# Five weight tiles carried together through the first normalization of a two-block transformer kernel

## The chip, the cores and the metric

One core of one Trainium2 chip runs the whole kernel as one launch. The metric is the device time of that launch in microseconds (us). The core's engines each work through their own queue in order: TensorE (PE, matmuls; PEld is its weight load), VectorE (DVE), ScalarE (ACT), GpSimd (POOL), and SyncE (SP), which issues the DMA transfers.

## The reference, cut to what matters

Two transformer blocks follow each other. The change touches only the entry of the first one: a vector `mod` of six parts is made from the condition `c`, two parts of it (`shift1`, `scale1`) turn the normalized input into `h`, and `h` is multiplied by the wide matrix `w_in`.

```python
mod = jax.nn.silu(c) @ w_ada[l] + b_ada[l]
shift1, scale1, gate1, shift2, scale2, gate2 = jnp.split(mod[:, None, :], 6, axis=-1)
h = rms_norm(x, norm1_w[l]) * (1 + scale1) + shift1
proj = h @ w_in[l]
(dn_q, dn_k, dn_v, dn_z, dn_alpha, dn_beta,
 mla_q, mla_ckv, mla_kr, gate_dn, gate_mla) = jnp.split(proj, split_at, axis=-1)
qkv = jax.nn.silu(causal_dwconv(jnp.concatenate([dn_q, dn_k, dn_v], axis=-1), dn_conv_w[l]))
...
```

There are 512 tokens (`T`) and 1024 features (`D`); all is float32. Behind the projection come a gated delta rule, a latent attention, a feed-forward part, and the second block. They take nearly all of the time and are not edited.

## The kernel before, in words

Features lie on the 128 partitions and tokens along the free dimension, so `x` and `h` are 8 slices (`KD`) of 128x512. Every product in float32 is made of two halves: `split` lets ScalarE round a tensor to `hi` (L294) and VectorE take the rest as `lo` (L295). `mm3` (L308 to L310) then issues three matmuls per slice: hi by hi, hi by lo, lo by hi. `proj` does that for the 8 slices of one weight tile, so one tile of 128 output features is 24 matmuls into one PSUM bank. `wload` fetches a tile of 128x1024 into `raw` (two buffers) and splits it. Two PSUM banks named `mm` are used in turn by all weight tiles.

The entry (the block with `w0`) works in this order:

1. `ssx`: the sum of squares of `x` on TensorE (L428), then `rstd` on ScalarE.
2. VectorE multiplies the 8 slices of `X0` by `rstd` (L433).
3. The modulation. `scale1` for slices 0 to 3 and `shift1` for slices 4 to 7 come from `cols_` on TensorE: a row of 512 outputs (L407, the vector is the stationary operand), copied by ScalarE (L410) and turned into columns by tiny matmuls (L413). The other half comes from `rows` on VectorE: one multiply-and-sum over 128x1024 for each block of 128 outputs (L397), eight in all.
4. `modulate`: ScalarE applies scale and shift to a slice (L420) and writes its `hi`, VectorE its `lo`. Slices 0 to 3 go first, then 4 and 5, then 6 and 7. The slices together are `H`.

Only two weight tiles, number 8 and `misc` (80 columns), are loaded inside this block. The first stage behind it (`t = 0`) projects tiles 8, 9, 0, 1, 16 and 17, each followed by `conv_silu`: ScalarE copies the PSUM bank (L527), VectorE adds three shifted products read from that bank (L529), ScalarE applies SiLU. The bank is free after the third product. `misc`, `ab` and `decay` make the decay terms (`aps` L480, `gps` L500). The next stage (`pre_steps`) begins with `gb`, `kk` and `ssp` on TensorE.

The order in which each engine gets its instructions is decided by the framework's scheduler from the order of the code, the buffers and its own costs. On the chip each engine keeps that order and waits where it must.

## Time and profile before

| what | value |
|---|---|
| median of three runs | 2167.57 us (2164.92 to 2167.89) |
| the profiled execution, its own time | 2166.97 us |
| its span, first to last instruction | 2165.2 us |
| TensorE busy | 2135.2 us, 99% |
| VectorE busy | 1202.5 us, 56% |
| ScalarE busy | 898.0 us, 41% |

A busy TensorE is not one at full speed: an interval also counts as busy while slow or small matmuls run in it. The first 100 us are the part that the change touches; TensorE is busy for 87.54 us of them.

### The profile page before, as it was taken

The numbers are of one execution on the slowest core, as the hardware profiler recorded it, in microseconds if no ns is written. First come the engines' busy times: TensorE is split into PE (matmuls) and PEld (weight loads), VectorE is DVE, ScalarE is ACT, GpSimd is POOL, SyncE is SP. The second block draws the span as 40 slices with busy tenths as digits, with TensorE's granted clock in tenths as the row PEclk, the third lists the DMA queues.
The fourth block names the chain that finished last, engine by engine and source line by source line (L and its number), as shares of the span: only waits on it lengthen the run. The fifth ranks groups of instructions, "written<-read, shape, count | busy, mean of one in ns | idle before, by whom it ended". The sixth has DMA issues, their size and how long they took to land.

```text
span 2165.2 us, 27498 instructions
## 1 busy us (share of the span) xinstructions
PE 2135.2 (99%) x10636; PEld 1722.0 (80%) x10636; DVE 1202.5 (56%) x2243; ACT 898.0 (41%) x1479; POOL 17.8 (1%) x49
## 2 busy tenths in 40 slices
PE   7999999999999999999999999999999999999997
PEld 3787877778888878888888887887778888888886
DVE  4777667465554554444335898545544454334446
ACT  5645443465553353333224323634443343224333
POOL 1000000000000000000000000000000000000000
PEclk9999999999999999999999999999999999999999
DMA  8533334222224343333333222232222433333332
GB/s 312 167 109 115 90 91 131 61 67 69 73 71 129 105 136 94 96 95 95 95 100 117 80 83 83 74 98 83 84 78 82 148 97 98 96 98 97 92 96 77
DMA packets 89579, 219.86 MB, mean 102 GB/s; under 512 B 23384, under 2 KB 28648, under 8 KB 88808
## 3 DMA queue, kind: packets, MB, share of 16 engines
q1 hardware_dynamic: 89448, 218.10, 33.0%
q8 instruction: 84, 1.38, 0.3%
q14 instruction: 47, 0.39, 0.1%
HBM read 211.50 MB, written 7.08 MB: 101 GB/s over the span
## 4 chain that ended last, share of the span: by engine, by line
PE 90%; DVE 5%; ACT 2%; issue 1%; DMA 1%; SPq 0%; DVEq 0%; ACTq 0%
PE mm L308 25%; PE mm L310 25%; PE mm L309 24%; PE pp L689 2%; DVE yc L1265 1%; DVE lo L295 1%; PE bpo L1593 1%; PE po L1041 1%; PE tps L1202 1%; PE tps L1203 1%; PE tps L1204 1%; PE ssp L571 1%; PE pw L762 1%; PE pc L789 1%; PE ss L779 1%
## 5 line engine op out<-in xcount | busy, mean ns | idle before, releaser
L294 ACT ACTIVATE hi<-raw 128x1024 fp32r<-128x1024 f32 (+3 forms) x354 | 351.5, 994 | 779.0 <-PE mm L309 690.4
L295 DVE TENSOR_TENSOR lo<-raw,hi 128x1024 fp32r<-128x1024 f32 (+3 forms) x354 | 403.8, 1141 | 439.0 <-ACT hi L294 427.9
L308 PE MATMUL mm<-H,hi 128*128 128x512 f32 x856 | 341.8, 400 | 4.7 <-ACT hi L294 1.7
L310 PE MATMUL mm<-H,lo 128*128 128x512 f32 (+1 forms) x856 | 340.5, 398 | 0.5 <-DVE lo L295 0.5
L309 PE MATMUL mm<-H,hi 128*128 128x512 f32 (+1 forms) x856 | 340.0, 397 | 0.0
L308 PEld LDWEIGHTS mm<-H,hi 128*128 128x128 f32 x856 | 161.4, 189 | 41.2 <-issue 3.0
L310 PEld LDWEIGHTS mm<-H,lo 128*128 128x128 f32 (+1 forms) x856 | 161.4, 189 | 36.1 <-issue 3.4
L309 PEld LDWEIGHTS mm<-H,hi 128*128 128x128 f32 (+1 forms) x856 | 161.5, 189 | 33.9 <-issue 2.7
L308 PE MATMUL mm<-XN,hi 128*128 128x512 f32 (+1 forms) x456 | 180.0, 395 | 0.0
L309 PE MATMUL mm<-XN,hi 128*128 128x512 f32 (+1 forms) x456 | 179.6, 394 | 0.0
L310 PE MATMUL mm<-XN,lo 128*128 128x512 f32 (+1 forms) x456 | 179.3, 393 | 0.0
L310 PEld LDWEIGHTS mm<-XN,lo 128*128 128x128 f32 (+1 forms) x456 | 85.1, 187 | 19.3 <-issue 1.7
L308 PEld LDWEIGHTS mm<-XN,hi 128*128 128x128 f32 (+1 forms) x456 | 85.1, 187 | 18.8 <-ACT hi L294 0.9
L309 PE MATMUL mm<-HN,hi 128*128 128x512 f32 x256 | 100.0, 391 | 0.0
L308 PE MATMUL mm<-HN,hi 128*128 128x512 f32 x256 | 99.6, 389 | 0.0
L310 PE MATMUL mm<-HN,lo 128*128 128x512 f32 x256 | 99.6, 389 | 0.0
L308 PE MATMUL mm<-F,hi 128*128 128x512 f32 x256 | 99.6, 389 | 0.0
L309 PE MATMUL mm<-F,hi 128*128 128x512 f32 x256 | 99.6, 389 | 0.0
L310 PE MATMUL mm<-F,lo 128*128 128x512 f32 x256 | 99.6, 389 | 0.0
L309 PEld LDWEIGHTS mm<-XN,hi 128*128 128x128 f32 (+1 forms) x456 | 84.9, 186 | 17.8 <-issue 1.3
L1265 DVE SCALAR_TENSOR_TENSOR yc<-cp,cdh,yc 128x512 f32<-128x512 f32 x120 | 89.9, 750 | 2.9
L308 PE MATMUL mm<-FF,hi 128*128 128x512 f32 x176 | 68.5, 389 | 0.0
(662 smaller groups left out, 3817.1 us busy)
## 6 DMA issues: line engine op xcount, KB each, us to landing
raw<-in_w_ff SPq DMA_DIRECT2D x64, 512.0 KB, 3.6
raw<-in_ffn_up SPq DMA_DIRECT2D x44, 512.0 KB, 3.6
raw<-in_w_dn SPq DMA_DIRECT2D x32, 512.0 KB, 3.8
adraw<-in_w_adaT SPq DMA_DIRECT2D x64, 256.0 KB, 3.2
raw<-in_w_ga SPq DMA_DIRECT2D x32, 512.0 KB, 3.7
raw<-in_w_br SPq DMA_DIRECT2D x32, 256.0 KB, 2.7
raw<-in_ffn_down SPq DMA_DIRECT2D x16, 448.0 KB, 3.4
X<-in_xT SPq DMA_DIRECT2D x4, 1024.0 KB, 7.2
```

The lines of the kernel that those rows point to most:

```text
L294: nc.scalar.activation(out=hi, in_=src, func=AF.Copy)
L295: nc.vector.tensor_tensor(out=lo, in0=src, in1=hi.bitcast(F32), op=ALU.subtract)
L308: nc.tensor.matmul(ps, wh, xh, start=start, stop=False)
L309: nc.tensor.matmul(ps, wh, xl, start=False, stop=False)
L310: nc.tensor.matmul(ps, wl, xh, start=False, stop=stop)
L571: nc.tensor.matmul(ssp[64 * h:64 * h + 64, kind * 8 + c:kind * 8 + c + 1], sq[:, c], C("ones", 0, 1), start=True, stop=True)
L689: nc.tensor.matmul(pp[:, c4], lh[:, c4], rh[:, c4], start=True, stop=True)
L762: nc.tensor.matmul(pw[64 * h:64 * h + 64], st["wt"][b][:, c4, 64 * h:64 * h + 64], S[:, h], start=True, stop=True)
L779: nc.tensor.matmul(ss, st["kd"][b][64 * h:64 * h + 64, c4], vn[64 * h:64 * h + 64], start=True, stop=True)
L789: nc.tensor.matmul(pc[:, 0], ATT[(2 * p + b) % 4][:, c4], vn, start=True, stop=True)
L1041: nc.tensor.matmul(po[:, qs], VT[:, kb, hh], pT[:, kb * P:kb * P + P], start=(kb == 0), stop=(kb == qb))
L1265: i = nc.vector.scalar_tensor_tensor(out=ycs[m], in0=cps[m][:, s:s + T], scalar=cdh[:, m * 31 + s:m * 31 + s + 1], in1=ycs[m], op0=ALU.mul ...
```

## The change

It edits the entry block and the beginning of stage 0.

- The five tiles `FIRST` = 8, `misc`, 9, 0, 1 are loaded and split inside the entry block, into buffers of their own (`phi`, `plo`). Each has its own PSUM bank: two are the `mm` banks, three come from a new pool `pfirst`. The loop over slices is now outside and the loop over tiles inside, so each slice of `H` is multiplied into all five tiles.
- The modulation goes pair by pair of slices: for slices k and k+1 both scale and shift, then the multiplication by `rstd`, then `H`. `scale1` of slices 0 to 3 is made on TensorE as columns at once (`on_pe`: the weight block is the stationary operand, the vector the moving one, 8 matmuls to a block). The other twelve blocks are on VectorE (`on_dve`), one DMA each.
- The row of `c` (`crow`, 512 KB once spread over the partitions) is now fetched before the constants `CS` and the second half of `x`.
- Stage 0 no longer projects these five tiles; their convolutions are called ahead of the stage, which keeps tiles 16 and 17.

```diff
-    a["w_ada1"] = np.ascontiguousarray(wa[:, T:T + D].reshape(KD, P, D).transpose(1, 0, 2))
-    a["w_adaT"] = np.ascontiguousarray(np.delete(wa.T.reshape(12, 4, P, D), (1, 2), axis=0).reshape(40, P, D))
+    a["w_ada1"] = wtiles(wa[:, D:D + T])
+    a["w_adaT"] = np.ascontiguousarray(np.delete(wa.T.reshape(12, 4, P, D), 2, axis=0).reshape(44, P, D))
...
+        if own is None:
...
+        else:
+            hi = own.tile([P, CH], F32R, tag="phi", name="phi", bufs=len(FIRST))
+            lo = own.tile([P, CH], F32R, tag="plo", name="plo", bufs=len(FIRST))
...
+    FIRST = (8, "misc", 9, 0, 1)
+    dpx = ExitStack()
+    pst = dpx.enter_context(pool("pst", 1, PS))
+    ppre = dpx.enter_context(pool("ppre", 1, PS))
+    fpx = ExitStack()
+    pfirst = fpx.enter_context(pool("pfirst", 3, PS))
...
+        cb = w0.tile([P, D], F32, name="cb0")
+        nc.sync.dma_start(out=cb, in_=A["crow"].to_broadcast([P, D]))
         nc.sync.dma_start(out=CS, in_=A["consts"])
         nc.sync.dma_start(out=X0[:, 4:8], in_=A["xT"][:, 4:8])
...
+        def ad_tile():
+            return w0.tile([P, D], F32, tag="ad", name="ad", bufs=10)
+
+        def on_dve(j, m):
+            raw = ad_tile()
+            nc.sync.dma_start(out=raw, in_=A["w_adaT"][j])
+            nc.vector.tensor_tensor_reduce(out=raw, in0=raw, in1=cb, scale=1.0, scalar=0.0,
+                                           op0=ALU.mult, op1=ALU.add, accum_out=am[:, m:m + 1])
+
+        def on_pe(k):
+            raw = ad_tile().rearrange("p (k c) -> p k c", k=KD)
+            nc.sync.dma_start(out=raw, in_=A["w_ada1"][k])
+            for kk in range(KD):
+                nc.tensor.matmul(adc[:, k:k + 1], raw[:, kk], csil[:, kk:kk + 1], start=(kk == 0), stop=(kk == KD - 1))
...
+        def first_w(i):
+            if i == "misc":
+                W0[i] = wload(A["w_misc"], KD, 80, w0)
+            else:
+                W0[i] = wload(A["w_dn"][i], KD, P, w0)
+            PS0[i] = (PSM[0] if len(PS0) < 2 else pfirst).tile([P, T], F32, tag="mm", name="mm")
...
+        for k in range(0, KD, 2):
+            for kk in (k, k + 1):
+                if kk < 4:
+                    on_pe(kk)
+                else:
+                    on_dve(4 + kk, 8 + kk)
+                on_dve(kk, kk)
+            if k == 0:
+                first_w(FIRST[0])
+                first_w(FIRST[1])
+            elif k // 2 + 1 < len(FIRST):
+                first_w(FIRST[k // 2 + 1])
+            mods(k)
+            for kk in (k, k + 1):
+                nc.vector.tensor_tensor(out=X0[:, kk], in0=X0[:, kk], in1=rstd, op=ALU.mult)
+                nc.scalar.activation(out=X0[:, kk], in_=X0[:, kk], func=AF.Identity, scale=s1[:, kk:kk + 1],
+                                     bias=mod[:, kk:kk + 1])
+                split(X0[:, kk], H[0][:, kk], H[1][:, kk])
         for k in range(KD):
-            nc.vector.tensor_tensor(out=X0[:, k], in0=X0[:, k], in1=rstd, op=ALU.mult)
-        cols_(T, 8)
...
+            for i in FIRST:
+                o = PS0[i][:80] if i == "misc" else PS0[i]
+                mm3(o, W0[i][0][:, k], W0[i][1][:, k], H[0][:, k], H[1][:, k], k == 0, k == KD - 1)
...
+    pj0 = proj_steps(0)
+    pj0[0]()
+    misc()
+    for f in pj0[1:len(FIRST) - 1]:
+        f()
+    fpx.close()
...
-        g0 = [misc, ab, decay] if t == 0 else []
+        g0 = [ab, decay] if t == 0 else []
```

The three `mm3` lines, L308 to L310 before, are L312 to L314 after. In the lists of instructions below, a bracket names what an instruction waits for: an engine, or a DMA queue (`DMAHW`); the numbers behind the names are buffer or semaphore numbers.

On TensorE, the entry before, from the first modulation block on (`adrow` is a row of outputs, `adcol` its turn into columns, `mm` the weight tiles):

```order
L407 MATMUL adrow<-ad_135,csil 1x512 [waits DMAHW5_49]
L407 MATMUL adrow<-ad_135,csil 1x512 x3
L407 MATMUL adrow<-ad_141,csil 1x512 [waits DMAHW6_49]
L407 MATMUL adrow<-ad_141,csil 1x512 x3
L413 MATMUL adcol<-CS,adrow_147 128x1 [waits Activation_49]
L413 MATMUL adcol<-CS,adrow_147 128x1 x3
L407 MATMUL adrow<-ad_179,csil 1x512 [waits DMAHW1_49]
L407 MATMUL adrow<-ad_179,csil 1x512 x3
L407 MATMUL adrow<-ad_185,csil 1x512 [waits DMAHW2_49]
L407 MATMUL adrow<-ad_185,csil 1x512 x3
L308 MATMUL mm<-H,hi 128x512 [waits Activation_49]
L309 MATMUL mm<-H,hi 128x512 [waits DVE_49]
```

The same place after (`adc` holds the columns, one block of 8 matmuls for each of slices 0 to 3):

```order
L415 MATMUL adc<-csil,ad 128x1 [waits DMAHW5_49]
L415 MATMUL adc<-csil,ad 128x1 x7
L415 MATMUL adc<-csil,ad 128x1 [waits DMAHW7_49]
L415 MATMUL adc<-csil,ad 128x1 x7
L415 MATMUL adc<-csil,ad 128x1 [waits DMAHW3_49,DVE_49]
L415 MATMUL adc<-csil,ad 128x1 x7
L312 MATMUL mm<-H,phi 128x512 [waits Activation_49]
L312 MATMUL mm<-H,phi 80x512
L313 MATMUL mm<-H,phi 128x512 [waits DVE_49]
L314 MATMUL mm<-H,plo 128x512
L313 MATMUL mm<-H,phi 80x512
L314 MATMUL mm<-H,plo 80x512
```

Rows and their turning are gone; three blocks of columns stand ahead of the first weight matmul, the fourth follows behind the matmuls of slice 0, and the third waits for VectorE to have read the first two.

On VectorE, the entry before, from the start of the program:

```order
L433 TENSOR_TENSOR X_87<-X_87,rstd 128x512 [waits DMAHW1_49,Activation_49]
L433 TENSOR_TENSOR X_87<-X_87,rstd 128x512 x3
L433 TENSOR_TENSOR X_87<-X_87,rstd 128x512 [waits DMAHW3_49]
L433 TENSOR_TENSOR X_87<-X_87,rstd 128x512 x3
L397 ISA ad_155,am_96<-ad_155,cb_93 128x1024 [waits DMAHW7_49]
L397 ISA am_96 128x1
L397 ISA ad_155,am_96<-ad_155,cb_93 128x1024
L397 ISA am_96 128x1
L414 TENSOR_TENSOR mod<-adcol,VS 128x4 [waits DMAHW0_49,PE_49]
L399 TENSOR_TENSOR mod<-am_96,VS 128x2 [waits DVE_49]
```

The same place after:

```order
L408 ISA ad,am_96<-ad,cb_89 128x1024 [waits DMAHW6_49,Activation_49]
L408 ISA am_96 128x1
L408 ISA ad,am_96<-ad,cb_89 128x1024 [waits DMAHW0_49]
L408 ISA am_96 128x1
L420 TENSOR_TENSOR mod<-adc,VS 128x2 [waits PE_49]
L418 TENSOR_TENSOR mod<-am_96,VS 128x2 [waits DVE_49]
L455 TENSOR_TENSOR X_87<-X_87,rstd 128x512 [waits DMAHW1_49,Activation_49]
L421 SCALAR_TENSOR_TENSOR s_61<-mod,VS 128x2 [waits DVE_49]
L455 TENSOR_TENSOR X_87<-X_87,rstd 128x512 x2
L295 TENSOR_TENSOR plo<-raw,phi 128x1024 [waits DMAHW1_49,Activation_49]
L295 TENSOR_TENSOR plo<-raw,phi 128x640 [waits DMAHW2_49,Activation_49]
L295 TENSOR_TENSOR H<-X_87,H 128x512 [waits Activation_49]
```

Before, the eight multiplications by `rstd` (L433) stand first and wait for ScalarE alone. After, two blocks of the modulation and the reading of the TensorE columns (L420, waits for PE) stand ahead of the first of them (L455), and nothing behind it can pass.

On TensorE, the fifth tile (number 1, weights `phi` and `plo`) after the change; ahead of these rows stand the matmuls of slices 0 to 5 for the other four tiles:

```order
L312 MATMUL mm<-H,phi 128x512 [waits Activation_49]
L313 MATMUL mm<-H,phi 128x512
L314 MATMUL mm<-H,plo 128x512
L312 MATMUL mm<-H,phi 128x512
L313 MATMUL mm<-H,phi 128x512
L314 MATMUL mm<-H,plo 128x512
L314 MATMUL mm<-H,plo 128x512 [waits DVE_49]
```

The last row is the first use of that tile's `plo` and waits for VectorE; it and 45 more matmuls follow before the five tiles are complete. Before, a tile's matmuls stand together, 24 in a row.

On VectorE, the convolutions of the first tiles after the change (`cacc` is the accumulator, 511, 510 and 509 columns are the three products of one tile; `plo` and `lo` splits are ahead of them):

```order
L544 SCALAR_TENSOR_TENSOR cacc<-mm,VS,cacc 128x511 [waits Activation_49]
L544 SCALAR_TENSOR_TENSOR cacc<-mm,VS,cacc 128x510 [waits DVE_49]
L544 SCALAR_TENSOR_TENSOR cacc<-mm,VS,cacc 128x509 [waits DVE_49]
L666 COPY UK<-DC 64x256 [waits DMAHW0_49]
L544 SCALAR_TENSOR_TENSOR cacc<-mm,VS,cacc 128x511 [waits Activation_49]
L544 SCALAR_TENSOR_TENSOR cacc<-mm,VS,cacc 128x511 [waits DVE_49,Activation_49]
L544 SCALAR_TENSOR_TENSOR cacc<-mm,VS,cacc 128x510 [waits DVE_49] x2
L544 SCALAR_TENSOR_TENSOR cacc<-mm,VS,cacc 128x509 [waits DVE_49] x2
L499 TENSOR_SCALAR beta<-beta 128x32 [waits Activation_49]
L500 TENSOR_TENSOR al<-aps,VS 128x32
```

The products of four tiles now stand close together, where before each tile's three stood between weight splits and other work.

## Rows read from the trace of the kernel before

**Rows 1.** Page, first line: length of the profiled execution.
```profile
span 2165.2 us, 27498 instructions
```

**Rows 2.** Windows: busy us of PE, PEld, DVE, ACT, POOL, then granted clock, DMA, GB/s.
```profile
30.00:40.00 10.00, 7.76 (x22) 4.46 (x21) 6.47 (x10) 4.84 (x8) 0.00 (x0) 0.76 0.73 268
...
100.00:200.00 100.00, 100.00 (x618) 80.59 (x617) 76.41 (x203) 51.12 (x99) 2.10 (x4) 1.00 0.40 119
```

**Rows 3.** Chain of waits, 0 to 160 us: start, us until the next step, what.
```profile
7.30 9.14 PE ssx L428 x16
...
16.43 6.97 PE adrow L407 x16
...
24.07 1.06 PE adcol L413 x8
...
26.52 1.14 DVE ad L397
...
27.78 1.52 ACT X L420 x2
...
29.30 1.04 ACT H L294 x2
...
36.11 1.81 PE adcol L413 x8
...
44.36 1.23 DVE lo L295
...
53.49 0.23 PE mm L308
...
58.28 1.03 PE aps L480 x32
...
68.83 0.82 PE gps L500 x8
...
69.87 0.67 DVE cacc L529
...
70.60 1.28 ACT L270
...
71.89 0.64 ACT KQ L270
```

**Rows 4.** Timeline of VectorE, 0 to 75 us: start, us, instruction.
```profile
17.85 4.91 DVE L433 TENSOR_TENSOR X<-X,rstd 128x512 f32<-128x512 f32 x8 [17.85 <-ACT rstd L264]
...
40.62 0.16 DVE L417 SCALAR_TENSOR_TENSOR s<-mod,VS 128x2 f32<-128x2 f32 x1
...
47.77 1.29 DVE L295 TENSOR_TENSOR H<-X,H 128x512 fp32r<-128x512 f32 x2 [2.11 <-ACT H L294]
```

**Rows 5.** Timeline of TensorE: first instruction after the seventh weight tile.
```profile
84.13 1.82 PE L571 MATMUL ssp<-CS,dsq 128*64 128x1 f32 x32
```

**Rows 6.** Timeline of TensorE: two neighbouring matmuls of the first weight tile.
```profile
38.42 0.63 PE L310 MATMUL mm<-H,lo 128*128 128x512 f32 x1
...
38.85 0.63 PE L308 MATMUL mm<-H,hi 128*128 128x512 f32 x1
```

**Rows 7.** Windows: granted clock (after POOL) before, in and after the slow stretch.
```profile
32.00:34.00 2.00, 0.28 (x2) 0.21 (x2) 1.53 (x3) 2.00 (x4) 0.00 (x0) 1.00 0.86 344
...
36.00:38.00 2.00, 2.00 (x10) 1.95 (x10) 0.06 (x1) 0.00 (x0) 0.00 (x0) 0.50 1.00 287
...
42.00:43.00 1.00, 1.00 (x6) 0.66 (x5) 1.00 (x3) 1.00 (x3) 0.00 (x0) 0.96 0.46 172
```

**Rows 8.** DMA queues, 0 to 70 us: GB/s in 40 slices, then issues by line.
```profile
GB/s 1 258 398 409 410 293 296 406 412 410 412 403 386 389 385 404 408 410 410 101 70 372 260 201 180 199 213 321 266 261 323 360 267 286 247 191 235 228 28 210
...
cb<-in_crow SPq DMA_DIRECT2D x2, 512.0 KB, 7.3
...
CS<-in_consts SPq DMA_DIRECT2D x1, 131.0 KB, 5.3
```

**Rows 9.** Timeline, SyncE queue: issue of the constants.
```profile
1.65 0.43 SPq L384 DMA_DIRECT2D CS<-in_consts  x1
```

More of the change, by code (lines that the diff above doesn't have):

```diff
@@ L375, in _body @@
     rctx = ExitStack()
-    oap = rctx.enter_context(pool("oap", 1, side="right"))
-    kqp = rctx.enter_context(pool("kqp", 3, side="right"))
-    PRE = {}
-    with pool("st0", 4, PS) as pst, pool("w0", 1) as w0:
+    FIRST = (8, "misc", 9, 0, 1)
[4 more added lines that the diff above has]
+    pfirst = fpx.enter_context(pool("pfirst", 3, PS))
+    PS0 = {}
+    with pool("w0", 1) as w0:
         nc.sync.dma_start(out=VS, in_=A["vecs"])
@@ L387, in _body @@
         acts(func=AF.Silu, out=csil, in_=V("c", 0, 8))
-        cb = w0.tile([P, D], F32, name="cb0")
-        nc.sync.dma_start(out=cb, in_=A["crow"].to_broadcast([P, D]))
         acts(func=AF.Silu, out=cb, in_=cb)
-        am = w0.tile([P, 8], F32, name="am0")
-        def rows(j, m):
-            raw = w0.tile([P, 2, D], F32, tag="ad", name="ad2", bufs=6)
-            nc.sync.dma_start(out=raw, in_=A["w_adaT"][j:j + 2].rearrange("j p k -> p j k"))
-            for q in range(2):
-                nc.vector.tensor_tensor_reduce(out=raw[:, q], in0=raw[:, q], in1=cb, scale=1.0, scalar=0.0,
-                                               op0=ALU.mult, op1=ALU.add, accum_out=am[:, j + q:j + q + 1])
-            nc.vector.tensor_tensor(out=mod[:, m:m + 2], in0=am[:, j:j + 2], in1=V("b_ada", m, 2), op=ALU.add)
@@ L401, in cols_ @@
-        def cols_(c0, m):
-            ps = pst.tile([P, T], F32, tag="st", name="adrow")
-            for q in range(2):
-                raw = w0.tile([P, 4, T], F32, tag="ad", name="ad4", bufs=6)
-                nc.sync.dma_start(out=raw, in_=A["w_ada1"][:, 4 * q:4 * q + 4, c0:c0 + T])
-                for k in range(4):
-                    nc.tensor.matmul(ps[0:1], csil[:, 4 * q + k:4 * q + k + 1], raw[:, k],
-                                     start=(q + k == 0), stop=(q == 1 and k == 3))
-            row = w0.tile([1, T], F32, tag="adrow", name="adrow0", bufs=2)
-            nc.scalar.activation(out=row, in_=ps[0:1], func=AF.Copy)
-            pc = pst.tile([P, T], F32, tag="st", name="adcol")
-            for i in range(4):
-                nc.tensor.matmul(pc[:, i:i + 1], row[:, i * P:i * P + P], C("ones")[0:1, 0:1], start=True, stop=True)
-            nc.vector.tensor_tensor(out=mod[:, m:m + 4], in0=pc[:, 0:4], in1=V("b_ada", m, 4), op=ALU.add)
@@ L416, in modulate @@
-        def modulate(k0, k1):
-            nc.vector.scalar_tensor_tensor(out=s1[:, k0:k1], in0=mod[:, 8 + k0:8 + k1], scalar=1.0,
-                                           in1=V("norm1_w", k0, k1 - k0), op0=ALU.add, op1=ALU.mult)
-            for k in range(k0, k1):
-                nc.scalar.activation(out=X0[:, k], in_=X0[:, k], func=AF.Identity, scale=s1[:, k:k + 1],
-                                     bias=mod[:, k:k + 1])
-                split(X0[:, k], H[0][:, k], H[1][:, k])
+        am = w0.tile([P, 16], F32, name="am0")
@@ new lines, in _body @@
+        adc = ppre.tile([P, T], F32, tag="pre", name="adc")
+        def ad_tile():
[10 more added lines that the diff above has]
+                nc.tensor.matmul(adc[:, k:k + 1], raw[:, kk], csil[:, kk:kk + 1], start=(kk == 0), stop=(kk == KD - 1))
@@ new lines, in mods @@
+        def mods(k):
+            nc.vector.tensor_tensor(out=mod[:, k:k + 2], in0=am[:, k:k + 2], in1=V("b_ada", k, 2), op=ALU.add)
+            src = adc if k < 4 else am[:, 8:16]
+            nc.vector.tensor_tensor(out=mod[:, 8 + k:10 + k], in0=src[:, k:k + 2], in1=V("b_ada", 8 + k, 2), op=ALU.add)
+            nc.vector.scalar_tensor_tensor(out=s1[:, k:k + 2], in0=mod[:, 8 + k:10 + k], scalar=1.0,
+                                           in1=V("norm1_w", k, 2), op0=ALU.add, op1=ALU.mult)
@@ L431, in _body @@
         actf(AF.Exp, out=rstd, in_=rstd, scale=-0.5)
-        for k in range(KD):
-            nc.vector.tensor_tensor(out=X0[:, k], in0=X0[:, k], in1=rstd, op=ALU.mult)
-        cols_(T, 8)
-        rows(0, 0)
-        rows(2, 2)
-        modulate(0, 4)
-        cols_(0, 4)
-        PRE[8] = wload(A["w_dn"][8], KD, P)
-        PRE["misc"] = wload(A["w_misc"], KD, 80)
-        for j in range(4, KD, 2):
-            rows(j, 8 + j)
-            modulate(j, j + 2)
+        for k in range(0, KD, 2):
[16 more added lines that the diff above has]
+                split(X0[:, kk], H[0][:, kk], H[1][:, kk])
+        for k in range(KD):
+            for i in FIRST:
+                o = PS0[i][:80] if i == "misc" else PS0[i]
+                mm3(o, W0[i][0][:, k], W0[i][1][:, k], H[0][:, k], H[1][:, k], k == 0, k == KD - 1)
+    oap = rctx.enter_context(pool("oap", 1, side="right"))
+    kqp = rctx.enter_context(pool("kqp", 3, side="right"))
     OA = oap.tile([P, KD, T], F32, tag="oab", name="OA")
@@ L470, in misc @@
     def misc():
-        mps = proj(PRE.pop("misc"), H, m=80)
+        mps = PS0.pop("misc")
         nc.scalar.activation(out=krraw, in_=mps[0:64], func=AF.Copy)
```

20 lines of the change are left out of this document (9 added, 11 removed).

## The prediction

> **What bounds the kernel now.** I first read the page and the windows. TensorE is the bound: between 100 and 200 us it is busy all the time at full clock while VectorE has a quarter of its time free [rows 2]. From there on the change edits nothing, so it can only move the moment at which this stretch begins. The window from 30 to 40 us shows what there is to win: TensorE is busy for 7.76 of 10 us at a mean clock of 0.76 [rows 2].
>
> The chain of waits [rows 3] tells what the entry consists of: `ssx` for 9.14 us, a row `adrow` of 6.97 us (there are two), `adcol` twice, then VectorE blocks of 1.14 us, ScalarE and VectorE work on `H`. The last slices of `H` get their `lo` from 47.77 us on [rows 4], and only then do weight tiles run without a break. My mark for "the same work done" is the end of the seventh weight tile (8, `misc`, 9, 0, 1, 16, 17): before, `ssp` starts right behind it at 84.1 us [rows 5].
>
> **The change part by part.** I follow the engines' queues in the order printed above, with durations from the trace. All times are us from the span's start.
>
> *Start of ssx.* The constants are issued at 1.65 and take 5.3, so they land at 6.95; `ssx`, which reads them, starts at 7.30 [rows 3, 8, 9]. Now 512 KB of `crow` go ahead of them; at about 400 GB/s [rows 8] that is 1.3 us, if transfers are served in the order of issue. Then `ssx` starts at 8.3 and ends at 17.4: 1.0 us lost. Bounds: 0 and 1.3.
>
> *Blocks on TensorE.* Both rows and `adcol` go: about 17 us of TensorE in a time when it had nothing better to do. Four blocks of 8 matmuls come, each with 128x128 weights and one moving column. No row shows that shape. The nearest is `gps`: 128x128 weights, 32 columns, 4 matmuls that the trace counts as 8 passes in 0.82, so 0.103 a pass [rows 3]. A block is then 16 passes, 1.65. `adcol` (one column too, but weights of one partition) gives 0.13 a pass at full clock and 0.23 in the slow stretch [rows 3], so the bounds are 1.65 and 3.6. I take `gps`, for its weights. Blocks 0 and 1 directly follow `ssx`, at full clock: done at 20.7.
>
> *The first new wait.* VectorE's first reading of these columns stands ahead of the multiplications by `rstd`, which started at 17.85 before [rows 4]; queued behind it are the whole of `H` and the weight splits. From 20.7 VectorE does three small operations (0.16 each), three multiplications (4.91 / 8 = 0.61 each) [rows 4], the `lo` of tile 8 (1.23) [rows 3] and of `misc` (80/128 of that) and the `lo` of slice 0 (half of 1.29) [rows 4]: 5.0, so 25.7. ScalarE's part beside it (1.52 and 1.04 for two slices [rows 3]) is shorter.
>
> *The second new wait.* Block 3 stands on TensorE behind the matmuls of slice 0, four of which need that `lo`. VectorE's next reading, and with it slices 2 to 7, waits for block 3. What this costs hangs on the clock. [...] After the change TensorE has only one-column blocks and waits between 17.4 and 25.7, so I take the slow clock: 4 x 0.43 + 16 x 0.206 = 5.0, block 3 ends at 30.7. At full clock it would be 0.9 + 1.65, ending at 28.3.
>
> *VectorE to the fifth tile.* From 30.7 to the `lo` of tile 1 its queue holds nine blocks (1.14 each, 10.3), four multiplications (2.5), three weight splits (3.7), four `lo` of `H` (2.6) and nine small operations (1.4): 20.5, so 51.2. The last two slices follow within three us. The four blocks that moved here from TensorE are 4.6 of this. Transfers are not in the way: the modulation is 8 MB as before; the first 15 transfers (8.05 MB) land at about 23 at some 380 GB/s [rows 8]. The load of tile 9 waits for the split of tile 8 (24.3), and behind it in SyncE's queue stand eight blocks and tile 0; these 5.2 MB land by 38; the last block is used at about 48. Were that cover of 10 us gone, each us late would be a us of the sum.
>
> *End of the five tiles.* 46 matmuls wait for the `lo` of tile 1, all others having been caught up on the way: 46 x 0.23 = 10.6, so 61.8.
>
> *Behind the five tiles.* Tiles 16 and 17 with `aps` (1.03 [rows 3]) take 48 x 0.23 + 1.03 = 12.1 on TensorE: 73.9. The next tile needs the bank of tile 16, and VectorE must now do five convolutions in a heap: three products for tile 8 (0.67 each [rows 3]) from 61.8 on, a wait for ScalarE's table load (1.28), SiLU (0.64) and copy (about as long), then twelve products (8.0), three half blocks (1.7) and small ones (0.5): 76.6. TensorE idles for 2.7. Before `gps` VectorE has another half block, a weight split, a product and two small ones, 2.8; `gps` itself takes 0.82: 80.2. By then TensorE has done six matmuls (1.4) that lie behind the mark; before had done `gb` and `kk` ahead of it, four passes (the two of `gb` at most 9.14 / 16 each), about the same.
>
> *Sum.* 84.1 - 80.2 = 3.9 us earlier. What follows keeps it, if VectorE does: it enters the next stage about as far as before, and has a quarter of its time free after 100 [rows 2]; I put 0 on this and 2 as a bound. The profiled execution took 2166.97 (its span of 2165.2 [rows 1] and 1.8 around it), 0.6 under the median of 2167.57. Against the median the forecast is 2163.7 us.
>
> **The rivals.**
>
> *A: more is gained.* If the clock holds, block 3 ends 2.4 earlier; if the constants are not held up, 1.0; if VectorE's heap is worked off beside TensorE, 2.7. All three together give a gain of 10.0, 2157.6; two of them about 2160. For it: the clock held through both rows, which also use the array thinly. Against it: `adcol`, the one row with a single moving column, did not bring the clock back [rows 7].
>
> *B: slower, by the clock.* The place is the last 46 matmuls. If they come 0.43 apart, they take 19.8 instead of 10.6, and 9.2 more turns the gain into a loss of 5.3: 2172.9. Each slow one costs 0.20, so it is slower than the measurement can miss (8.2 of the sum gone) from 41 of the 46 on. Against it: they wait for nothing long, and before, with two tiles in turn, the clock was back at 0.96 in the window from 42 to 43 [rows 7]. [...]
>
> *C: the gain is given back.* The five convolutions in a heap and the ScalarE table loads between them delay `kk` and `ssp`, so that TensorE waits for these instead. VectorE's share beyond 100 us speaks against a long delay [rows 2]; with the 2 us of the bound and half a us more in each of the next few tiles the time is 2165 to 2169.
>
> *That the change does not do what it says*, the five tiles being done when `H` is, is in the forecast already: the fifth weight's `lo` stands so late on VectorE that 46 of the loop's 120 matmuls come behind it.
>
> **How the numbers follow.** A difference below 0.2% (4.3 us) can't be told from none here. Forecast, 2162 to 2166: 0.52, a little more than half of it within 4.3 us. A, 2157.5 to 2161: 0.23. C: 0.18, mostly without a measurable change. B: 0.07. Faster: 0.23 and 0.22 of the forecast, 0.45. Slower: B and the end of C, 0.10. The rest, 0.45, is the same. The range from 2158 to 2168.5 leaves out B and the ends of A and C, under 0.2; the forecast's own is 2162 to 2166.
>
> **What would show it.** In the new profile: `ssx` from 8.3; the second block of columns done near 20.7 and VectorE idle until then; a granted clock of 0.50 when the fourth block runs, done near 30.7; the `lo` of the fifth tile near 51 and the five tiles done near 62; TensorE idle for some 3 us around 75; `gps` done near 80. I am wrong if block 3 ends before 29 (then A), if the last matmuls of the five tiles are 0.43 apart (B), or if TensorE idles for more than 2 us between 80 and 100 (C).

## The result, and the profile after

The changed kernel is slower: 2182.23 us in the median of 4 runs (2180.46 to 2184.32) against 2166.85 of 4 (2164.92 to 2167.89), a ratio of 1.0072 with a 95% interval of 1.0055 to 1.009. That is 15.4 us, outside the predicted range. The profiled execution took 2183.33 us, its span is 2181.6, against 2165.2 [rows 1]. Four executions that took far longer than all others of the same kernel (5.4 ms in `dc_own_queue` and in `cs_first`, 2358.65 and 9605.16 us in the kernel before) are left out of every number below.

The entry itself gained time. TensorE's projection matmuls (output `mm`) of the first 65 us, in the windows of the kernel before:

```profile
0.00:65.00 65.00, 26.23 (x97) 18.33 (x98) 4.44 (x6) 2.43 (x4) 0.95 0.86 304
```

and of the kernel after:

```profile
0.00:65.00 65.00, 33.81 (x121) 24.52 (x122) 0.86 (x2) 1.75 (x3) 0.84 0.74 274
```

The first pair behind the window is TensorE's busy time and count: 121 against 97. The 24 more are worth 24 x 0.23 = 5.5 us; `aps`, which before had done by then [rows 3] and after had not, takes 1.0 of it back. So the kernel after is some 4.5 us ahead at 65 us. This lead, and more, is then lost in two places. Windows of all instructions show them; first the kernel before (behind the five engines stand the granted clock, the DMA share and GB/s):

```profile
core 0: us, PE busy (x) PEld busy (x) DVE busy (x) ACT busy (x) POOL busy (x), PEclk, DMA share, GB/s
...
65.00:130.00 65.00, 64.54 (x380) 51.75 (x379) 53.25 (x127) 41.49 (x68) 0.00 (x0) 1.00 0.44 139
...
200.00:330.00 130.00, 129.66 (x820) 100.82 (x820) 85.32 (x263) 55.31 (x122) 3.16 (x6) 0.99 0.32 95
```

then the kernel after; a second fence has its stretches at half clock (0.50 in the column PEclk), one by one:

```profile
65.00:130.00 65.00, 58.18 (x344) 45.73 (x344) 46.13 (x108) 37.26 (x61) 1.26 (x3) 0.87 0.42 140
130.00:200.00 70.00, 70.00 (x423) 57.51 (x422) 52.46 (x143) 31.45 (x60) 1.57 (x3) 1.00 0.45 139
200.00:330.00 130.00, 129.64 (x782) 99.72 (x782) 89.18 (x287) 55.61 (x121) 2.63 (x5) 0.91 0.27 81
330.00:460.00 130.00, 130.00 (x794) 100.56 (x793) 76.91 (x211) 56.43 (x132) 1.57 (x3) 1.00 0.30 89
```

```profile
42.40:69.50 27.10, 24.69 (x106) 18.87 (x104) 17.17 (x30) 12.82 (x17) 5.34 (x11) 1.00 0.60 198
69.60:76.40 6.80, 5.92 (x42) 5.02 (x43) 3.50 (x6) 2.30 (x4) 0.00 (x0) 0.50 0.34 128
...
86.70:93.50 6.80, 5.98 (x18) 4.54 (x18) 5.95 (x16) 6.23 (x9) 0.00 (x0) 0.50 0.51 165
103.80:107.10 3.30, 3.30 (x9) 2.62 (x9) 3.26 (x9) 0.00 (x0) 0.00 (x0) 0.50 0.16 60
...
219.90:233.30 13.40, 13.40 (x67) 10.04 (x66) 6.70 (x29) 3.00 (x8) 0.00 (x0) 0.50 0.00 0
...
298.40:308.40 10.00, 10.00 (x51) 7.10 (x47) 4.12 (x15) 2.43 (x8) 0.00 (x0) 0.50 0.01 2
```

From 65 to 130 us TensorE idles for 6.8 us (before 0.5), and of its busy time 15.2 us lie at half clock (5.92 + 5.98 + 3.30), which costs half of that, 7.6, by an estimate (full matmuls come 0.43 apart in the first of these stretches and 0.23 behind it): together about 14. From 200 to 330 us it hardly idles, but the clock is 0.91 in place of 0.99; the two stretches of 13.4 and 10.0 cost 11.7, the kernel before loses 1.6 there. That is 24 us against the 4.5 of the lead, or 19.5; the spans differ by 16.4. The 3 us between are not assigned: the two programs do their other work in another order there.

The chain of waits of the kernel after shows what begins the first loss:

```profile
54.79 1.24 DVE lo L295
56.05 5.59 DMA raw<-in_w_dn
61.66 1.07 ACT hi L294
62.76 1.24 DVE lo L295
64.01 0.33 SPq L307
64.39 6.05 DMA DC<-in_dconsts
70.48 1.88 PE aps L495 x32
...
78.68 0.62 ACT KQ L270
79.32 0.70 ACT cacc L542
80.05 0.75 DVE cacc L544
80.89 0.59 DVE adraw L342
81.49 2.64 DVE cacc L544 x4
...
87.37 0.66 DVE cacc L544
88.28 1.89 PE gps L515 x8
```

The constants `DC` are issued at 64.39, because on SyncE's queue four weight loads stand ahead of them, and these wait for `raw` buffers, that is for VectorE's `lo`. `aps` reads `DC` and waits on TensorE until 70.48; everything on TensorE waits behind it. Then VectorE works off the heap of convolutions (`cacc`) that the five tiles, ending together, have left it, and `gps` runs at 88.28 where it ran at 68.83 [rows 3]. TensorE's own waits of after from 45 to 130 us say the same (in all, times, longest):

```profile
PE aps L495 <- DMA DC<-in_dconsts: 3.4, 1, 3.4
PE mm L312 <- DVE cacc L544: 2.6, 2, 2.2
PE gps L515 <- DVE G L508: 0.8, 1, 0.8
```

### The profile page after: what moved, and what is told of

Read it like the earlier page. It is cut to its first block, busy times and chain, and to the rows that moved or that the text cites. A ratio compares the mean times of both kernels' runs of the same rounds, so it can differ in the third digit from the quotient of the medians.

```text
span 2181.6 us, 27539 instructions
## 1 busy us (share of the span) xinstructions
PE 2146.8 (98%) x10652; PEld 1741.0 (80%) x10652; DVE 1208.0 (55%) x2254; ACT 895.6 (41%) x1477; POOL 18.0 (1%) x49
## 4 chain that ended last, share of the span: by engine, by line
PE 90%; DVE 6%; ACT 2%; issue 1%; DMA 1%; SPq 0%; DVEq 0%; ACTq 0%
PE mm L313 24%; PE mm L312 24%; PE mm L314 24%; PE pp L704 2%; DVE yc L1289 1%; PE bpo L1617 1%; DVE lo L295 1%; PE po L1065 1%; PE tps L1226 1%; PE tps L1227 1%; PE tps L1228 1%; PE ssp L586 1%; PE pw L777 1%; PE pc L804 1%; PE ss L794 1%
## 5 line engine op out<-in xcount | busy, mean ns | idle before, releaser
L294 ACT ACTIVATE hi<-raw 128x1024 fp32r<-128x1024 f32 (+4 forms) x349 | 346.7, 994 | 787.6 <-PE mm L313 691.4
L295 DVE TENSOR_TENSOR lo<-raw,hi 128x1024 fp32r<-128x1024 f32 (+4 forms) x349 | 398.2, 1141 | 436.0 <-ACT hi L294 425.2
L312 PE MATMUL mm<-H,hi 128*128 128x512 f32 x816 | 327.2, 401 | 3.4 <-DVE cacc L544 2.6
L313 PE MATMUL mm<-H,hi 128*128 128x512 f32 x816 | 327.5, 401 | 0.0
L314 PE MATMUL mm<-H,lo 128*128 128x512 f32 x816 | 327.2, 401 | 0.0
L312 PEld LDWEIGHTS mm<-H,hi 128*128 128x128 f32 x816 | 155.8, 191 | 37.6 <-issue 3.0
L313 PEld LDWEIGHTS mm<-H,hi 128*128 128x128 f32 x816 | 155.5, 191 | 33.4 <-issue 3.9
L314 PEld LDWEIGHTS mm<-H,lo 128*128 128x128 f32 x816 | 155.7, 191 | 33.0 <-issue 3.6
L312 PE MATMUL mm<-XN,hi 128*128 128x512 f32 (+1 forms) x456 | 180.0, 395 | 0.0
L314 PE MATMUL mm<-XN,lo 128*128 128x512 f32 (+1 forms) x456 | 179.3, 393 | 0.0
L314 PEld LDWEIGHTS mm<-XN,lo 128*128 128x128 f32 (+1 forms) x456 | 85.1, 187 | 19.3 <-issue 1.7
L312 PEld LDWEIGHTS mm<-XN,hi 128*128 128x128 f32 (+1 forms) x456 | 85.1, 187 | 18.9 <-ACT hi L294 0.9
L312 PE MATMUL mm<-HN,hi 128*128 128x512 f32 x256 | 99.6, 389 | 0.0
L314 PE MATMUL mm<-HN,lo 128*128 128x512 f32 x256 | 99.6, 389 | 0.0
L312 PE MATMUL mm<-F,hi 128*128 128x512 f32 x256 | 99.6, 389 | 0.0
L314 PE MATMUL mm<-F,lo 128*128 128x512 f32 x256 | 99.6, 389 | 0.0
L312 PE MATMUL mm<-FF,hi 128*128 128x512 f32 x176 | 68.5, 389 | 0.0
```

Source lines behind the costliest of these rows:

```text
L294: nc.scalar.activation(out=hi, in_=src, func=AF.Copy)
L295: nc.vector.tensor_tensor(out=lo, in0=src, in1=hi.bitcast(F32), op=ALU.subtract)
L312: nc.tensor.matmul(ps, wh, xh, start=start, stop=False)
L313: nc.tensor.matmul(ps, wh, xl, start=False, stop=False)
L314: nc.tensor.matmul(ps, wl, xh, start=False, stop=stop)
```

## The experiments

Before the first experiment I had three theories. **Q**: the late `DC` and what stands behind it make the loss. **E**: the entry itself does (late `CS`, columns at half clock). **O**: the half-clock stretches belong to TensorE's order of instructions and come whether or not something waits. The table has all runs. Idle is TensorE's between 65 and 130 us, and the last two columns are us at half clock (from 43 to 130, and from 130 to 330), all of the profiled run, whose time stands beside. Each ratio is to the kernel before in the same job. The half-clock columns and the idle time stand for one run of each program only, while the ranges show how far its runs spread.

| run | median us (range) | ratio, 95% | profiled | idle | half, early | half, late |
|---|---|---|---|---|---|---|
| before | 2166.85 (2164.92-2167.89) | | 2166.97 | 0.5 | 0 | 3.4 |
| after | 2182.23 (2180.46-2184.32) | 1.0072 (1.0055-1.009) | 2183.33 | 6.8 | 17.1 | 23.8 |
| modulation_alone | 2169.30 (2167.33-2171.49) | 1.0007 (0.9997-1.0017) | 2169.90 | 0.5 | 6.8 | 3.4 |
| five_tiles_alone | 2177.56 (2173.18-2179.31) | 1.0042 (1.0027-1.0057) | 2173.18 | 5.0 | 6.8 | 3.5 |
| dc_own_queue | 2178.00 (2169.04-2182.93) | 1.0047 (1.0033-1.006) | 2182.93 | 4.2 | 10.2 | 34.2 |
| cs_first | 2182.05 (2177.87-2182.39) | 1.006 (1.0043-1.0077) | 2182.39 | 6.9 | 13.6 | 24.0 |
| dc_early | 2176.28 (2170.66-2176.81) | 1.0038 (1.0023-1.0053) | 2170.66 | 6.7 | 17.0 | 0 |
| three_tiles | 2167.08 (2166.28-2169.18) | 1.0002 (0.9992-1.0011) | 2169.18 | 0.2 | 6.9 | 3.4 |
| three_tiles_dc_cs | 2167.55 (2165.81-2168.77) | 1.0004 (0.9995-1.0014) | 2167.97 | 0.2 | 6.8 | 3.4 |
| four_tiles | 2181.71 (2177.12-2183.64) | 1.0059 (1.0043-1.0074) | 2183.09 | 2.7 | 23.9 | 13.7 |
| four_tiles_dc_cs | 2182.60 (2180.58-2184.23) | 1.0069 (1.0055-1.0082) | 2180.58 | 2.7 | 17.1 | 10.2 |
| five_no_taps | 2171.57 (2164.19-2177.20) | 1.0019 (1.0007-1.0031) | 2170.08 | 1.8 | 10.2 | 3.4 |
| old_mod_three | 2173.50 (2172.10-2174.76) | 1.0028 (1.0018-1.0039) | 2174.76 | 0.6 | 13.6 | 3.5 |
| four_own_acc | 2178.23 (2177.91-2179.55) | 1.0053 (1.004-1.0065) | 2177.91 | 8.1 | 17.0 | 3.4 |
| five_own_acc | 2180.29 (2174.51-2183.15) | 1.0058 (1.0045-1.007) | 2183.15 | 4.8 | 13.7 | 34.0 |
| three_own_acc | 2174.25 (2171.84-2183.16) | 1.0038 (1.0024-1.0052) | 2175.38 | 0.2 | 6.8 | 17.0 |
| old_mod_three_own | 2170.90 (2169.67-2174.14) | 1.002 (1.0012-1.0029) | 2172.45 | 3.8 | 10.2 | 3.4 |
| filler_matmuls | 2192.30 (2191.44-2193.08) | 1.0118 (1.0101-1.0135) | 2192.29 | 4.1 | 20.5 | 10.2 |
| ssp_after_transposes | 2174.64 (2168.28-2177.28) | 1.0032 (1.0021-1.0044) | 2177.28 | 5.5 | 10.3 | 13.7 |
| three_own_dc_cs | 2170.55 (2162.58-2174.29) | 1.0011 (1.0001-1.0021) | 2162.58 | 0.3 | 6.8 | 0 |

### Either part alone

`modulation_alone` has the new modulation and the projection of the kernel before, `five_tiles_alone` the reverse. Both edits are shown in part, as differences from the kernel after:

```diff
-    FIRST = (8, "misc", 9, 0, 1)
+    FIRST = (8, "misc")
...
-        ps = PS0.pop(widx) if widx in PS0 else proj(A["w_dn"][widx], H)
+        ps = proj(W0.pop(widx, A["w_dn"][widx]), H)
```

```diff
-                if kk < 4:
-                    on_pe(kk)
-                else:
-                    on_dve(4 + kk, 8 + kk)
-                on_dve(kk, kk)
...
+        cols_(T, 8)
+        rows(0, 0)
+        rows(2, 2)
+        modulate(0, 4)
```

> One part of the change alone: the modulation blocks as in the changed kernel (by pairs, four of them on TensorE as columns), but the first projection as in the kernel before: two weight tiles loaded early, and tile after tile. DC then stands behind three weight loads in place of five. Theory Q (the loss is in what the five tiles do to the loads and waits behind them): the loss is not here, 2160 to 2170. Rival E (the columns at half clock and the late CS cost most): 2175 to 2185.

> The other part alone: five tiles advance together as H gets ready, with the modulation of the kernel before (four blocks at a time, two of the halves through a row on TensorE). DC stands on SyncE's queue behind four weight loads, as in the changed kernel. Theory Q: aps waits for DC again, half-clock stretches follow, and the time is 2174 to 2186. Rival E: the loss is gone, 2160 to 2170.

The modulation alone is not to be told from the kernel before; the five tiles alone cost 10 us. E falls: the columns at half clock (20 us at 0.50 in `after`, from 22 to 42) are there in both `modulation_alone` and `after` (a mean clock of 0.79 and 0.84 in the first 65 us), and the loss is there without them (`five_tiles_alone`, 0.95). In `five_tiles_alone` `aps` waits 1.3 us for `DC`, less than the 3.4 of the kernel after, and the waits for accumulators are 2.5 us. The two medians do not add up to after's 15.4.

### DC and CS

```diff
-    nc.sync.dma_start(out=DCt, in_=A["dconsts"])
+    nc.gpsimd.dma_start(out=DCt, in_=A["dconsts"])
```

> The changed kernel with one edit: the load of the constants DC is issued from GpSimd's queue, which is empty, where it stood on SyncE's queue behind four weight loads. The order on TensorE, VectorE and ScalarE stays, but for one matmul ahead of aps. Theory Q (the late DC is the start of the loss: TensorE stands 3.4 us at aps, and the half-clock stretches at 69.6 to 76.4 and 86.7 to 93.5 follow from that): aps starts at 64 to 67 in place of 70.5, both stretches go or shrink, and the time falls by 6 to 10 us, to 2172 to 2176. Rival E (the loss was made in the entry, by the late CS and the columns at half clock): DC gives under 2 us, 2180 to 2183. Rival O (the half-clock stretches are set by the order of the matmuls and not by the wait): 3 to 4 us, the wait alone, 2178 to 2179, with the two stretches still there. By Q and O alike the stretches at 219.8 to 233.4 and 298.3 to 308.5 stay, since the order there is the same.

`cs_first` puts the loads of `CS` and the second half of `X0` ahead of that of `cb` again:

> The changed kernel with the constants CS and the second half of X loaded ahead of the row cb again, as in the kernel before; every engine's order is otherwise the same. Theory Q: ssx starts 1.6 us earlier, at 7.3, but the DC load and aps are set by the weight loads behind VectorE's splits, which wait for the same queue of work: 0 to 1.5 us back, 2180.5 to 2182.5. Rival E (the entry's start is the loss and everything behind it moves with it): 1.5 to 4 us back, 2178 to 2180.7.

In `dc_own_queue` the wait for `DC` is gone, `aps` starts at 66.9 and the first `ssp` at 91.9 in place of 97.7. So early on Q is right: 3.4 us of wait brought 5.8. The median fell by 4.2 only (the intervals of the two ratios overlap), and the profiled run by nothing: from 200 us on it has stretches at half clock of 13.5 and 20.3 us.

```profile
214.30:227.80 13.50, 13.50 (x66) 10.20 (x67) 7.05 (x29) 3.00 (x8) 0.00 (x0) 0.50 0.00 0
292.80:313.10 20.30, 20.30 (x85) 13.72 (x84) 7.04 (x26) 3.33 (x12) 0.00 (x0) 0.50 0.00 1
```

`cs_first` starts `ssx` at 7.1 in place of 8.9, and no difference in the median follows. That 1.8 us is swallowed on the way: `DC` is issued at 64.06 in place of 64.39, and the wait for it is 3.8 us in place of 3.4.

`dc_early` loads `DC` into memory of its own, directly behind the load of the fifth weight tile (at 36.43 us in its trace, and not before that tile, as its expectation says); it also changes TensorE's order:

```diff
+    dcp = dctx.enter_context(pool("dcp", 1))
+    DCt = dcp.tile([P, NDCST], F32, name="DC")
...
+            if k == 6:
+                nc.sync.dma_start(out=DCt, in_=A["dconsts"])
```

> The changed kernel with DC in memory of its own, loaded before the fifth weight tile; this moves TensorE's order from about 65 us on (unlike dc_own_queue). Theory Q: no wait at aps, first kk and ssp as early as in dc_own_queue or earlier (92 or less). Theory O (the half-clock stretches at 214 to 233 and 293 to 313 belong to one order of TensorE's instructions, which dc_own_queue shares with the changed kernel, and eat what is gained in front of them): in this other order they are shorter, and the time is 2166 to 2174. Rival to O (they come whatever the order is): 2176 to 2182 as in dc_own_queue.

The wait for `DC` is gone, but TensorE now waits 6.2 us in one piece for VectorE's `G`. There is no late stretch in the profiled run (2170.66). The three others took 2176, with a mean clock of 0.987 to 0.988 against 0.990; where they lost it no trace shows.

### How many tiles

```diff
-    FIRST = (8, "misc", 9, 0, 1)
+    FIRST = (8, "misc", 9)
```

> The changed kernel with three tiles advancing together (8, misc, 9) in place of five; the other two follow one after another as in the kernel before. Theory Q (the loss at 60 to 130 us is a chain of waits behind five tiles that end together: two more weight tiles in front of DC on the queue, then two more convolutions at once on VectorE, so that matmuls wait for accumulators and gps for G): the wait for accumulators (2.6 us in two) falls under 1 us, gps comes by 80 in place of 88.3, half-clock stretches between 65 and 110 shrink, and the time is 2170 to 2176. Rival E: nothing changes, 2179 to 2184.

> Three tiles, DC from GpSimd's queue and CS ahead of cb, all together. Theory Q: each takes away its own wait (1.6 us at ssx, 3.4 at aps, 2 at the accumulators): 2163 to 2172. If theory O holds and the order keeps the late half-clock stretches: 2170 to 2178.

> The changed kernel with four tiles advancing together (8, misc, 9, 0); one size between three_tiles (2167.1) and the changed kernel (2182.2). Theory Q in its form after three_tiles (five tiles that end together give VectorE four convolutions at once while TensorE needs their accumulators, and put two weight loads ahead of DC): with four, three convolutions fall together, the loss shrinks but stays, 2169 to 2176. Rival (it is the order of TensorE further on alone that makes 2167 or 2182, by chance of the schedule): no step between, either within 2 us of 2167 or within 2 us of 2182.

> Four tiles, DC from GpSimd's queue, CS ahead of cb. Theory Q: against four_tiles the wait for DC is gone if there was one, and ssx starts 1.6 us earlier: 1 to 5 us less than four_tiles. Rival (as with three tiles, where both edits changed nothing: 2167.55 against 2167.08): within 1.5 us of four_tiles.

This one line takes all the loss away: 2167.08, no difference from the kernel before. Between 65 and 130 us the waits for `DC`, for accumulators and for `G` are gone (idle 0.2; ahead of 65 TensorE waits 1.2 us for the copy of `misc`), and of the stretches 6.9 and 3.4 us are left. `DC` and `CS` bring nothing on top, since with three tiles TensorE does not wait for `DC`. With four tiles it is as slow as with five. In `four_tiles` TensorE waits from 45 us on for

```profile
PE mm L312 <- ACT mab L488: 4.2, 1, 4.2
PE mm L312 <- DVE t L507: 2.7, 1, 2.7
```

that is for ScalarE's copy of `misc` (which frees an accumulator) and for VectorE. My form of Q with `DC` in the middle falls here, since nothing in this list waits for `DC`; the wait is at another place each time. What VectorE has to do was tried by leaving out work: `five_no_taps` is `dc_own_queue` without nine shifted products of the convolutions of tiles 9, 0 and 1 (these outputs are then not the reference's).

```diff
-        for s in range(1, 4):
+        for s in range(1, 1 if widx in (9, 0, 1) else 4):
```

> dc_own_queue (five tiles, DC from GpSimd's queue) without the three shifted convolution steps of tiles 9, 0 and 1: nine VectorE instructions of 0.66 us, 5.9 us of work, are left out, so these three outputs are not the reference's. Theory Q (VectorE's heap of convolutions is what TensorE waits for at 78 to 88 us): the waits for accumulators (3.3 us in two) and for G (0.9) fall under 1 us, gps comes at 76 or earlier in place of 82.3, the half-clock stretch at 81 to 88 goes, and the work done by 130 us is that of the kernel before or more. The time falls to 2164 to 2172 if the order further on does not bring stretches of its own. Rival (the wait is for ScalarE or the accumulators' number): gps stays at 81 to 83 and the time at 2175 to 2180.

The waits for the products (3.3 us in `dc_own_queue`) are gone, `gps` starts at 78.4 (82.3) and the median falls by 6.4. The late stretches are also shorter in its profile, so how much of the 6.4 is the heap's stays open. `old_mod_three` is the old modulation with three tiles and `DC` on GpSimd's queue:

> A version put together from the parts: three tiles advance together, the modulation of the kernel before (no columns at half clock), DC from GpSimd's queue. Theory Q: the start of the projection is as early as in five_tiles_alone (18 matmuls more done by 65 us there than in the kernel before) and nothing is given back behind it: 2162 to 2166. Rival (the gain of the start is taken back by waits further on, as in three_tiles): 2166 to 2169.

It does not bring what Q expected: TensorE waits 5.9 us for the copy of `misc`, and a stretch at half clock from 57.3 to 64.1 follows.

### Accumulators

All these waits could be one: the joint tiles hold both accumulators of the pool that the next tiles use. Theory **P** gives the joint tiles their own (in `five_own_acc` four of the five, so that one of the pool's two is free).

```diff
-    pfirst = fpx.enter_context(pool("pfirst", 3, PS))
+    pfirst = fpx.enter_context(pool("pfirst", 4, PS))
...
-            PS0[i] = (PSM[0] if len(PS0) < 2 else pfirst).tile([P, T], F32, tag="mm", name="mm")
+            PS0[i] = pfirst.tile([P, T], F32, tag="mm", name="mm")
```

> four_tiles with all four joint tiles in accumulators of their own, so that both buffers of the pool that the following tiles use are free. Theory P (the accumulators are the wait): the waits of 4.2 us for the copy of misc and 2.7 us for VectorE go, the half-clock stretches between 60 and 110 us shrink from 24 us to under 12, and the time falls from 2181.7 to 2166 to 2174. Rival (the work of VectorE and ScalarE behind the joint tiles sets it): waits move to the next tiles or to gps and kk, 2177 to 2183.

> dc_own_queue with four of the five tiles in accumulators of their own and the first in one of the pool's two, so that one buffer is free for the sixth tile; TensorE's order is that of the changed kernel but for 20 lines. Theory P: the wait for accumulators (3.3 us) falls to under 1 us, first kk and ssp at 89 to 90 in place of 91.9; the time falls by 2 to 5 us below dc_own_queue (2178.3), unless the late half-clock stretches eat it. By theory O those late stretches (214 to 228, 293 to 313) stay, since the order stays: 2172 to 2178. Rival: no change, 2177 to 2181.

> three_tiles with its three joint tiles in accumulators of their own. There TensorE waits 1.2 us for the copy of misc and 2.2 us for H in ScalarE. Theory P: 1 to 3 us less than three_tiles (2167.1), 2164 to 2166.5, and with that below the kernel before. Rival: the gain goes into a wait for VectorE or for weights, 2166.5 to 2169.

> old_mod_three with its three joint tiles in accumulators of their own. There TensorE waited 5.9 us for ScalarE's copy of misc, and a half-clock stretch followed at 57 to 64. Theory P: the wait and the stretch go, 5 to 9 us less than old_mod_three (2173.5), 2164 to 2168. Rival: under 2 us less, 2171 to 2174.

P falls for four and five tiles. In `four_own_acc` the two waits are gone, and in their place stand

```profile
PE gps L515 <- DVE G L508: 5.6, 1, 5.6
PE aps L495 <- DMA DC<-in_dconsts: 3.2, 1, 3.2
```

TensorE runs ahead into the next thing that VectorE and SyncE's queue have not ready. In `five_own_acc` the wait does not even move:

```profile
PE mm L312 <- DVE cacc L544: 4.8, 2, 4.4
```

In `dc_own_queue`, from which it is made, that line had 3.3 us. `old_mod_three_own` gains 2.6 us, under the 5 to 9 of P. `three_own_acc` idles little and has 6.8 us at half clock by 130, but then stretches of 3.4 and 13.6, and 2174.

### The late stretches

After, `dc_own_queue`, `cs_first` and `five_own_acc` share TensorE's order there, and all have a stretch of about 13.6 us that begins within three matmuls of the same place, though they reach it up to 6 us apart. TensorE's timeline of the kernel after where that stretch begins:

```profile
216.54 1.82 PE L586 MATMUL ssp<-CS,dsq 128*64 128x1 f32 x32
218.29 0.50 PE L312 MATMUL mm<-H,hi 128*128 128x512 f32 x1
218.72 0.44 PE L777 MATMUL pw<-S,wt 128*64 128x128 f32 x4
219.09 0.50 PE L313 MATMUL mm<-H,hi 128*128 128x512 f32 x1
219.43 0.70 PE L656 MATMUL tpv<-CS,vf 128*128 128x128 f32 x4
220.06 0.69 PE L784 MATMUL pc<-S,KQ 128*64 128x128 f32 x4
```

The one-column `ssp` of a pair of heads stands among the transposes (`tpv`) of the pair ahead and steps of the recurrence (`pw`, `pc`); few matmuls of 512 columns lie between. In the kernel before, `ssp` comes behind those transposes, with full matmuls around.

The order is not the whole cause, though. `five_tiles_alone` has it too: the 1640 matmuls that the kernel after runs between 130 and 400 us stand in its trace in the same order. Its profiled run keeps a clock of 0.99 there:

```profile
200.00:330.00 130.00, 128.38 (x822) 99.05 (x821) 87.98 (x280) 56.77 (x124) 2.63 (x5) 0.99 0.27 81
```

It has one stretch, which begins 8 to 11 matmuls earlier in that order, directly behind `ssp`, and is over 3.4 us later, among the very steps in which the others stay slow (`ss` is back at 0.49; it took 0.80 in `dc_own_queue` and `cs_first`):

```profile
213.44 1.82 PE L590 MATMUL ssp<-CS,dsq 128*64 128x1 f32 x32
215.19 0.77 PE L312 MATMUL mm<-H,hi 128*128 128x512 f32 x1
...
217.10 1.06 PE L660 MATMUL tpv<-CS,vf 128*128 128x128 f32 x4
...
218.72 0.49 PE L798 MATMUL ss<-vn,kd 64*128 64x128 f32 x4
```

So O falls as it was put: one and the same order came with 3.5 us at half clock from 130 us on and with 23.8 to 34.2. What decides beside the order is open.

Two runs tried the order itself. `filler_matmuls` puts full ones in, `ssp_after_transposes` changes the order alone:

```diff
+                    if c % 4 == 3:
+                        nc.tensor.matmul(ssp[:, 64:512], H[0][:, s, 0:P], H[1][:, s, 64:512], start=True, stop=True)
```

```diff
+                    if p > 0:
+                        after(i, ST[p - 1]["tv"])
```

> dc_own_queue with 32 more matmuls of 448 columns, two in each group of 16 one-column ssp matmuls, into columns of the same PSUM tile that nothing reads; TensorE's work grows by 32 x 0.2 = 6.4 us. Theory O (the stretches at half clock at 214 to 228 and 293 to 313 start in the groups of small matmuls, where TensorE is occupied but little runs in it): with full matmuls among them the stretches go or shrink; they cost 17 us in the profiled run of dc_own_queue, so the time falls to 2168 to 2175 in spite of the added work. Rival (the stretches have another cause): 6 us more than dc_own_queue, 2183 to 2187.

> dc_own_queue with one rule of order more: the 32 ssp matmuls of a pair of heads come on TensorE behind the last transpose (tpv) of the pair ahead. No work is added or left out. Theory O (long half-clock stretches come from ssp among transposes and recurrence steps, where little runs on TensorE): the stretches at 214 to 228 and 293 to 313 shrink to under 7 us each, the time falls from 2178.3 to 2165 to 2172 and the runs spread less than the 14 us of dc_own_queue. Rival (the stretches have another cause, or ssp coming later makes a wait of its own): 2176 to 2182 with stretches of 10 us and more.

`filler_matmuls` settles nothing: the stretch at 214 is gone and a later one stays, the rest of the order moved too, and a filler among one-column matmuls holds TensorE for 0.39 us (one starts at 221.03, the next instruction at 221.42) and not 0.20, so that 32 of them cost some 12 us (an estimate, 32 x 0.39). In `ssp_after_transposes` each of the two long stretches became two short ones:

```profile
219.10:222.30 3.20, 3.20 (x11) 1.86 (x10) 0.97 (x4) 0.00 (x0) 0.00 (x0) 0.50 0.01 4
225.90:229.10 3.20, 3.20 (x8) 2.55 (x9) 2.98 (x15) 0.90 (x2) 0.00 (x0) 0.50 0.17 14
297.60:300.80 3.20, 3.20 (x8) 1.95 (x8) 0.33 (x2) 2.09 (x5) 0.00 (x0) 0.50 0.25 97
304.40:307.70 3.30, 3.30 (x9) 2.62 (x9) 3.04 (x16) 0.97 (x3) 0.00 (x0) 0.50 0.00 0
```

34 us at half clock became 14, which O expected; the profiled run is 5.7 us faster than that of `dc_own_queue`, the median 3.4, less than O's 6 to 13, and the intervals of the two ratios overlap. As one order gave anything from 3.5 to 34.2 us, one profiled run with 14 does not show that the order shapes these stretches; it is only compatible with it.

> Three joint tiles in accumulators of their own, DC from GpSimd's queue, CS ahead of cb; the order of TensorE further on is its own again. By theory Q and the early part of three_own_acc (2.7 us less lost by 130 us than three_tiles) and of cs_first (1.5 us): 2162 to 2166 if the late stretches stay at 3 to 7 us. If ssp falls among the transposes again, as in three_own_acc: 2168 to 2176.

The profiled run has no late stretch and takes 2162.58, less than any run of the kernel before in these jobs (2164.42). The other ten runs of the same program lie between 2164.14 and 2174.29, and the median is not below the kernel before. No version beats it.

## Why the prediction was wrong

- **Start of ssx** (8.3, end 17.4): 8.88, end 19.0. The row on the path is `CS`, issued at 2.13 and 6.62 long, and `ssx` itself took 10.14, not 9.14. Together 1.6 us under-sized.
- **Blocks on TensorE** (two blocks done at 20.7): 23.0, of which 1.6 were there before. The price of a pass was right: the line below has 27 in 2.68 us at full clock, 0.099 each, where 0.103 was taken. But the clock fell within the second block and not behind it: 1.00 up to 21.70, 0.50 from 22.2. Block 3 ended at 32.9 (30.7); it ran at half clock, as forecast, its 16 passes in 3.40 us at 0.50. The 0.43 in its sum is the distance of two matmuls in the slow stretch before [rows 6, 7]; here too three in a row came 0.43 apart ahead of block 3, from 28.24 to 29.52.

```profile
19.02:21.70 2.68, 2.68 (x27) 2.68 (x26) 0.00 (x0) 1.00 1.02 405
```

- **VectorE to the fifth tile** (`lo` done at 51.2): its split ran from 51.13 to 52.4. Here the working was about right (19.4 us where 20.5 were taken), from a start 2.2 us late.
- **End of the five tiles** (61.8): 64.8. When the fifth `lo` was done 53 matmuls were left, not 46, which is 1.6 of the 3.0 us. They came 0.23 apart at a clock of 1.00, so rival B's place was wrong.
- **Behind the five tiles** (`gps` done at 80.2): 90.2. This is the first step whose mechanism failed; those above are only mis-sized. Of the 10.0 us, 3.0 were there at the end of the five tiles, and 7.0 came here. The working gave `aps` 1.03 and took its constants as loaded: `DC` was not in the sum, because I had followed SyncE's queue only as far as the fifth tile. Four weight loads stand ahead of it there, which wait for VectorE's splits. It cost 3.4 us of wait, and what followed ran at half clock: `aps` 1.88 in place of 1.03, the matmuls behind it 0.43 apart up to 76.5, `gps` 1.89 in place of 0.82 [rows 3]. The VectorE heap was in the sum, with an idle of 2.7; it was 2.6 at the accumulators and 0.8 at `G`, about as sized, but behind it came a second stretch at half clock (86.7 to 93.5), which I had not priced.
- **Sum, "what follows keeps it"** (0, at most 2): the second failed step, about 10 us. It was judged by VectorE's free time beyond 100 us [rows 2]. What went wrong there is not a wait: between 200 and 330 us TensorE was busy for 129.64 of 130, at a clock of 0.91. The sum had no term for the clock there. The changed entry also gives TensorE another order up to about 480 us, which I took as without price; but `five_tiles_alone` has this order from 130 to 400 us at a clock of 0.99 from 200 to 330, so that the order alone does not explain it.
- **Rivals.** B suspected the clock, but at the last 46 matmuls, which ran at 1.00. C had the heap and the table loads, priced at 2 us, and its sign did show: TensorE idled for 3.0 us between 80 and 90. Neither reaches 2182.

At `DC` TensorE waited 3.4 us, up to 70.48, and the granted clock was 0.50 from 69.6 to 76.4. The five tiles' matmuls, over five banks in turn, ran at 1.00 from 42.4 to their end at 64.8.

Shown: five joint tiles cost what is lost and three do not (2182.2, 2167.1). The late `DC` makes a part of it (`ssp` comes 5.8 us earlier without it; the median falls by 4.2, with intervals that overlap), the convolutions' work another (at most 6.4); accumulators of their own win little or nothing back. Argued: that the half-clock stretches early on follow from these waits. Open: why four tiles are as slow as five, and what makes the late stretches, some 10 of the lost us; the order of TensorE alone does not.
